# Issuing the gated linear attention's score products for two levels at a time

## The chip, the cores and the metric

The kernel runs on one core of one Trainium2 chip. The metric is the time of one execution on the device, in microseconds (us); the times given are medians of several runs.

## The reference

Two layers of an encoder on 256 tokens of width 2048. Each layer has one input projection, three groups of heads that work side by side, one output projection, and a gated MLP with a depthwise convolution. The change touches one group only, the gated linear attention (GLA): four heads with keys of 64 and values of 128, run forward and backward and added.

```python
def gla_direction(q, k, v, log_a):
    ...
    cum = jnp.cumsum(log_a.astype(F32).reshape(b, h, n, c, dk), axis=3)
    pair = jnp.where(lower[:, :, None],
                     jnp.exp(jnp.minimum(cum[..., :, None, :] - cum[..., None, :, :], 0.0)), 0.0)
    scores = jnp.einsum('bhnik,bhnjk,bhnijk->bhnij', q, k, pair.astype(q.dtype))
    intra = jnp.einsum('bhnij,bhnjv->bhniv', scores, v)
    ...
la_f = split_heads(jax.nn.log_sigmoid((ga_f @ gate_w[0] + gate_b[0])...) / GLA_TAU, GLA_HEADS)
o = gla_direction(q, k, v, la_f) + flip_t(gla_direction(flip_t(q), flip_t(k), flip_t(v), flip_t(la_b)))
```

So the score of a pair of tokens (i, j) is the product of q_i and k_j, weighted in each channel by the exponential of the summed log gates between them.

## The kernel before

**Slots.** All weights are read as a list of slots, one block of some 128 output columns each. For every slot the main loop (`for s in range(4, NS + 1)`) does the same: ScalarE (ACT) makes a rounded copy of a weight block that is needed three slots later (`split_hi`, line 176), VectorE (DVE) makes the remainder of a block that is needed two slots later (`split_lo`, line 184), TensorE (PE) multiplies this slot's block (lines 202 and 204 for the slots named rq, rk, dq, dk and others; 24 products on lines 218 to 220 for the slots gv, rv, dv), and the result is evacuated: ACT line 225 and DVE line 226 first, then, in the rq and rk slots, the rotary embedding (lines 394 to 401). The order in a layer is gv0 to gv3, ga, gq, gk, gq, gk, rq0, rq1, rk0, rk1, rv0 to rv3, dv0 to dv3, eight slots of dq and dk, and so on. In the first layer rk1 is slot 12, rv0 to rv3 are slots 13 to 16 and dv0 to dv2 are slots 17 to 19; the names are used below for both layers.

**Side tasks.** The heads' work lies in generators. `run_tasks` lets each active one go on to its next `yield`. GLA is an "early" task, so it makes one step at the head of a slot (`run_tasks(0, (True,))`, ahead of the splits and the slot's products) and one at its tail (`run_tasks(1)`, behind the products and behind the slot's evacuation). Others make their first step of a slot behind the splits. GLA counts 2 of the 3 places for active tasks; the tasks behind it in the list wait until it ends. In the first layer `decay_strips` runs beside it in slots 12 to 18 (lines 721 to 726).

**Order.** The schedule is the program's own order: each engine works through its instructions in the order in which the program issues them, and waits by semaphores for the other engines.

**GLA.** The scores are built in eight levels, with blocks of b = 1, 2, 4, ... 128 tokens. A level needs: `exps(b)`, two or four exponentials on ACT (lines 513 to 517) from four running sums, into the tiles `ea` and `eb`; two products on DVE, `ea = q*ea` (line 555) and `eb = k*eb` (line 557, not at b = 1); eight small products on PE into two banks (`scores`, line 539); and two predicated copies on DVE from those banks into `mm` (line 564; at b = 128 two copies on ACT, line 572). `update(b)`, four additions on DVE (line 524), makes the sums of the next level. One level takes two steps:

```python
                dve.tensor_mul(ea, q, ea)
                if b > 1:
                    dve.tensor_mul(eb, k, eb)
                yield
                bk = scores(k if b == 1 else eb, ea, b == P)
                if b < P:
                    update(b)
                    exps(2 * b)
```

The first `yield` of level 1 falls at the head of slot rk1, so the eight score blocks stand at the tails of rk1, rv0, ... dv2, one per slot. The final products (lines 584 and 587) follow.

Of the kernel before, what the change touches and what calls it, by code (L numbers as in the profile page):

```python
# [20 lines left out]
P = 128  # L21
T = 256
# [77 lines left out]
def encoder_kernel(ctx: ExitStack, tc: tile.TileContext, wflat, xT, par, con, masks, gate_w, lam_p, rel_bias, decay, out):  # L100
    nc = tc.nc
    pe, act, dve, pool = nc.tensor, nc.scalar, nc.vector, nc.gpsimd
# [7 lines left out]
    big = Slots(rot, "big", 36, 512)  # L110
# [247 lines left out]
    class Mixer:  # L358
# [98 lines left out]
        def gla(self):  # L457
# [3 lines left out]
            pf, sb, sfx, pbx = (big.get() for _ in range(4))  # L461
# [17 lines left out]
            for pr in range(2):  # L479
                act.activation(ab[pr], ab[pr], AF.Exp, scale=-1.0)  # L480
            yield
            q, k, ea, eb = (big.get() for _ in range(4))
            mm = [big.get() for _ in range(2)]
            for pr in range(2):
                for d, src in ((q, "gq"), (k, "gk")):
# [7 lines left out]
            bk, d = [banks.get() for _ in range(2)], tny.get()  # L493
# [15 lines left out]
            def V(a, b):  # L509
                return a.rearrange("p (n w b) -> p n w b", w=2, b=b)  # L510

            def exps(b):
                act.activation(V(ea, b)[:, :, 1], V(pf, b)[:, :, 1], AF.Exp, scale=1.0 / TAU)
                act.activation(V(ea, b)[:, :, 0], V(sb, b)[:, :, 0], AF.Exp, scale=1.0 / TAU)
                if b > 1:
                    act.activation(V(eb, b)[:, :, 0], V(sfx, b)[:, :, 0], AF.Exp, scale=1.0 / TAU)
                    act.activation(V(eb, b)[:, :, 1], V(pbx, b)[:, :, 1], AF.Exp, scale=1.0 / TAU)

            def update(b):
                n = 256 // b  # L520
                lo, up = (lambda a: V(a, b)[:, :, 0]), (lambda a: V(a, b)[:, :, 1])

                def add(dst, src):
                    dve.tensor_add(dst, dst, src.to_broadcast([P, n, b]) if b > 1 else src)  # L524

                add(lo(sfx), up(pf)[:, :, b - 1:b])
                add(up(pbx), lo(sb)[:, :, 0:1])
                add(up(pf), lo(pf)[:, :, b - 1:b])
                add(lo(sb), up(sb)[:, :, 0:1])

            def scores(ks, qs, cross):
                bk = [banks.get() for _ in range(2)]
                for pr in range(2):
                    for jb in range(2):
                        ib = 1 - jb if cross else jb
                        for hp in range(2):
                            rows = slice(64 * hp, 64 * hp + 64)
                            c = (pr * 2 + jb) * P
                            pe.matmul(bk[hp][:, c:c + P], lhsT=ks[rows, c:c + P],  # L539
                                      rhs=qs[rows, (pr * 2 + ib) * P:(pr * 2 + ib + 1) * P], start=True, stop=True)  # L540
                return bk

            for pr in range(2):
                for d, dst in ((0, pf), (1, sb)):
                    sl = slice(d * T, (d + 1) * T)
                    dve.scalar_tensor_tensor(dst[:, pr * T:(pr + 1) * T], zs[pr][:, sl], 0.0, ab[pr][:, sl],
                                             ALU.min, ALU.subtract)
            big.put(*zs, *ab)
            exps(1)
            yield  # L550
            yield
            b = 1
            lev = 0
            while b < T:
                dve.tensor_mul(ea, q, ea)
                if b > 1:
                    dve.tensor_mul(eb, k, eb)
                yield
                bk = scores(k if b == 1 else eb, ea, b == P)
                if b < P:  # L560
                    update(b)
                    exps(2 * b)
                    for hp in range(2):
                        dve.copy_predicated(
                            mm[hp].rearrange("p (n i) -> p n i", i=P),
                            mask_t[:, lev:lev + 1, :].to_broadcast([P, 4, P]),
                            bk[hp].rearrange("p (n i) -> p n i", i=P))
                else:
                    big.put(pf, sb, sfx, pbx, ea, eb, q, k)
                    mo = [big.get() for _ in range(2)]  # L570
                    for hp in range(2):
                        act.activation(mo[hp], bk[hp], AF.Copy)
                banks.put(*bk)
                yield
                b *= 2
                lev += 1
            for pr in range(2):
                yield
                po = banks.get()
# [345 lines left out]
    for s in range(4, NS + 1):  # L925
        l, kind, i, c, _ = slots[min(s, NS - 1)]
# [50 lines left out]
        else:  # L977
            b = banks.get()
# [134 lines left out]
```

## Time and profile before

| | us |
|---|---|
| median of 3 runs | 2320.37 (2320.01 to 2320.68) |
| the profiled execution | 2320.66 |
| its span, first to last instruction | 2318.9 |
| PE, DVE, ACT busy | 2293.3, 1705.8, 1236.9 |

The span is what the trace holds; the profiled execution's own time is 1.76 us longer. Busy time of PE is the time in which a matrix product was under way, and their ends are modelled. In a timeline a row gives start, length, engine, line, operation, the tiles written and read, shapes and how many were merged (xN); in brackets the idle time of the engine before it and what ended that.

### The profile page before, as it was taken

The page shows a single profiled execution, that of the slowest core. Times are in us where ns is not written, and L with a number is a line of the kernel's source. Part 1 is how long each engine was busy: PE and PEld are TensorE (multiplying, and loading weights), DVE is VectorE, ACT ScalarE, POOL GpSimd, SP SyncE. Part 2 cuts the span into 40 slices and gives each one's busy share as a digit, 9 for nine tenths or more (in the row PEclk, how much of TensorE's full clock was granted, in tenths as well). Part 3 has the DMA queues.
Part 4 walks back from the last instruction along what each step waited for, and adds up shares of the span by engine and source line. Part 5 has one row for each costly group of instructions (what it writes and reads, how often), then busy time and mean ns, then how long its engine had stood idle before and what let it go on. Part 6 is the DMA issues. An engine that isn't in the chain of part 4 may idle for free.

```text
span 2318.9 us, 32791 instructions
## 1 busy us (share of the span) xinstructions
PE 2293.3 (99%) x13250; PEld 2013.3 (87%) x13250; DVE 1705.8 (74%) x2459; ACT 1236.9 (53%) x1769; POOL 62.3 (3%) x77
## 2 busy tenths in 40 slices
PE   8999999999999999999999999999999999999998
PEld 7888888888888888888888889888888888888887
DVE  7978886777577766777669788767775777567764
ACT  6557655555345533555445666545543555345553
POOL 0001100000000000000000111000000000000000
PEclk9999999999999999999999999999999999999999
DMA  7454445554555555555554444555555554555553
GB/s 284 176 176 162 163 168 191 186 187 172 192 200 184 194 180 189 197 182 186 189 184 165 154 164 156 182 193 182 187 177 200 184 197 176 187 199 183 191 177 105
DMA packets 66646, 423.10 MB, mean 182 GB/s; under 512 B 7960, under 2 KB 10904, under 8 KB 28096
## 3 DMA queue, kind: packets, MB, share of 16 engines
q1 hardware_dynamic: 66352, 420.96, 51.2%
q8 instruction: 104, 1.70, 0.3%
q14 instruction: 46, 0.38, 0.1%
q10 hardware_dynamic: 144, 0.06, 0.0%
HBM read 417.83 MB, written 2.11 MB: 181 GB/s over the span
## 4 chain that ended last, share of the span: by engine, by line
PE 89%; DVE 9%; ACT 1%; POOL 1%; issue 0%; DMA 0%; ACTq 0%; SPq 0%; DVEq 0%; POOLq 0%
PE bank L202 52%; PE bank L204 28%; DVE wts L184 2%; PE bank L218 2%; PE bank L219 2%; PE bank L220 2%; POOL tny L354 1%; DVE sml L232 1%; DVE sml L226 1%; PE bank L539 0%; DVE tny L644 0%; DVE big L642 0%; DVE sml L424 0%; DVE big L524 0%; DVE big L658 0%
## 5 line engine op out<-in xcount | busy, mean ns | idle before, releaser
L202 PE MATMUL bank<-big,wts 128*128 128x512 f32 x5760 | 1383.9, 392 | 8.4 <-DVE big L816 7.8
L202 PEld LDWEIGHTS bank<-big,wts 128*128 128x128 f32 x5760 | 1058.4, 188 | 217.1 <-DVE big L816 10.4
L176 ACT ACTIVATE wts<-wts 128x2048 fp32r<-128x2048 f32 (+3 forms) x398 | 744.2, 1870 | 308.8 <-PE bank L202 266.8
L184 DVE TENSOR_TENSOR wts<-wts,wts 128x2048 fp32r<-128x2048 f32 (+3 forms) x398 | 888.5, 2233 | 12.7 <-PE bank L219 8.4
L204 PEld LDWEIGHTS bank<-big,wts 128*128 128x128 f32 x5760 | 739.7, 191 | 28.4
L204 PE MATMUL bank<-big,wts 128*128 128x256 f32 x5760 | 748.6, 283 | 0.0
L890 DVE TENSOR_TENSOR x<-bank,x 128x256 f32<-128x256 f32 x256 | 108.7, 425 | 246.9 <-PE bank L204 242.5
L226 DVE TENSOR_TENSOR sml<-sml,bank 128x256 f32<-128x256 f32 (+1 forms) x242 | 101.8, 421 | 196.2 <-ACT sml L225 195.8
L225 ACT ACTIVATE sml<-bank 128x256 f32<-128x256 f32 (+1 forms) x242 | 92.0, 381 | 159.4 <-PE bank L204 159.2
L815 ACT ACTIVATE big<-sml 128x256 fp32r<-128x256 f32 x88 | 36.7, 417 | 190.8 <-DVE sml L813 190.8
L810 ACT ACTIVATE sml<-sml 128x256 f32<-128x256 f32 x88 | 36.8, 418 | 159.3 <-DVE sml L803 159.3
L218 PE MATMUL bank<-wts,big 128*128 128x512 f32 x256 | 103.3, 404 | 5.8 <-ACT wts L166 5.8
L801 ACT ACTIVATE sml<-sml,conv_t 128x256 f32<-128x256 f32 x176 | 103.4, 588 | 5.7 <-DVE sml L232 5.7
L232 DVE TENSOR_TENSOR sml<-sml,sml 128x256 f32<-128x256 f32 (+1 forms) x230 | 97.9, 426 | 7.9
L219 PE MATMUL bank<-wts,big 128*128 128x512 f32 x256 | 101.3, 396 | 0.0
L220 PE MATMUL bank<-wts,big 128*128 128x512 f32 x256 | 100.9, 394 | 0.0
L802 DVE SCALAR_TENSOR_TENSOR sml<-sml,conv_t,sml 128x255 f32<-128x255 f32 x176 | 84.3, 479 | 8.6 <-ACT sml L801 8.6
L803 DVE SCALAR_TENSOR_TENSOR sml<-sml,conv_t,sml 128x255 f32<-128x255 f32 x176 | 85.3, 485 | 6.3
L291 ACT ACTIVATE sml<-x 128x256 f32<-128x256 f32 x80 | 31.8, 415 | 77.1 <-DVE x L890 77.1
L816 DVE TENSOR_TENSOR big<-sml,big 128x256 fp32r<-128x256 f32 x88 | 37.4, 426 | 42.6 <-ACT big L815 42.6
L218 PEld LDWEIGHTS bank<-wts,big 128*128 128x128 f32 x256 | 48.8, 191 | 17.1 <-ACT wts L166 5.8
L220 PEld LDWEIGHTS bank<-wts,big 128*128 128x128 f32 x256 | 48.8, 191 | 10.4
(147 smaller groups left out, 1034.5 us busy)
## 6 DMA issues: line engine op xcount, KB each, us to landing
wts<-wflat SPq DMA_DIRECT2D x300, 1024.0 KB, 4.8
wts<-wflat SPq DMA_DIRECT2D x64, 960.0 KB, 4.7
wts<-wflat SPq DMA_DIRECT2D x32, 896.0 KB, 4.6
wts<-wflat SPq DMA_DIRECT2D x18, 256.0 KB, 5.7
x<-xT SPq DMA_DIRECT2D x8, 256.0 KB, 5.9
out<-big SPq DMA_DIRECT2D x8, 256.0 KB, 3.9
strips<-dr SPq DMA_DIRECT2D x1, 1536.0 KB, 8.7
sml<-sml SPq DMA_DIRECT2D x32, 32.0 KB, 1.9
```

The source lines that it names most:

```text
L176: act.activation(R(hi), raw, AF.Copy)
L184: dve.tensor_sub(R(lo), raw, hi)
L202: pe.matmul(pt, lhsT=R(hi[:, j * P:(j + 1) * P]), rhs=R(acts[j]), start=k == 0, stop=False)
L204: pe.matmul(pt[:, T:], lhsT=R(lo[:, j * P:(j + 1) * P]), rhs=R(acts[j][:, :T]), start=False, stop=k == n - 1)
L218: pe.matmul(pts[tb], lhsT=al, rhs=R(hi[:, w]), start=k == 0, stop=False)
L219: pe.matmul(pts[tb], lhsT=ah, rhs=R(lo[:, w]), start=False, stop=False)
L220: pe.matmul(pts[tb], lhsT=ah, rhs=R(hi[:, w]), start=False, stop=k == KB - 1)
L225: act.activation(t[:m], pts[0][:m, T:], AF.Copy)
L226: dve.tensor_add(d[:m], t[:m], pts[0][:m, :T])
L232: dve.tensor_mul(d[:m], d[:m], rb[:m])
L801: act.activation(c, us, AF.Identity, scale=w[1], bias=w[3])
L890: dve.tensor_add(xb[i], pts[0][:, h * T:(h + 1) * T], xb[i])
```

## The change

Two pairs of tiles take the place of `ea` and `eb`. Four iterations handle two levels each, in three steps: the first makes the first level's products with q and k, then `update` and `exps` of the second level into the other pair of tiles; the second step makes the second level's products; the third issues the score products of both levels, sixteen into four banks, then `update` and `exps` of the next pair's first level, then the predicated copies of both levels. The loop has 12 yields in place of 16. Every arithmetic instruction of before is still there, once.

```diff
-            q, k, ea, eb = (big.get() for _ in range(4))
+            q, k = big.get(), big.get()
+            es = [(big.get(), big.get()) for _ in range(2)]
...
-            def exps(b):
+            def exps(b, ea, eb):
...
-            exps(1)
-            yield
-            yield
-            b = 1
-            lev = 0
-            while b < T:
-                dve.tensor_mul(ea, q, ea)
-                if b > 1:
-                    dve.tensor_mul(eb, k, eb)
-                yield
-                bk = scores(k if b == 1 else eb, ea, b == P)
+            exps(1, *es[0])
+            yield
+            yield
+
+            def take(b, lev, bk):
                 if b < P:
-                    update(b)
-                    exps(2 * b)
                     for hp in range(2):
                         dve.copy_predicated(
...
                 else:
-                    big.put(pf, sb, sfx, pbx, ea, eb, q, k)
-                    mo = [big.get() for _ in range(2)]
                     for hp in range(2):
                         act.activation(mo[hp], bk[hp], AF.Copy)
                 banks.put(*bk)
+
+            for lev in range(0, 8, 2):
+                b = 1 << lev
+                for i in range(2):
+                    ea, eb = es[i]
+                    dve.tensor_mul(ea, q, ea)
+                    if b << i > 1:
+                        dve.tensor_mul(eb, k, eb)
+                    if i == 0:
+                        update(b)
+                        exps(2 * b, *es[1])
+                    yield
+                bks = [scores(k if b << i == 1 else es[i][1], es[i][0], b << i == P) for i in range(2)]
+                if 2 * b < P:
+                    update(2 * b)
+                    exps(4 * b, *es[0])
+                else:
+                    big.put(pf, sb, sfx, pbx, *es[0], *es[1], q, k)
+                    mo = [big.get() for _ in range(2)]
+                for i in range(2):
+                    take(b << i, lev + i, bks[i])
                 yield
-                b *= 2
-                lev += 1
```

## Rows read from the trace of the kernel before

**Rows 1.** The page, busy time and share of the span.
```profile
PE 2293.3 (99%) x13250; PEld 2013.3 (87%) x13250; DVE 1705.8 (74%) x2459; ACT 1236.9 (53%) x1769; POOL 62.3 (3%) x77
```
**Rows 2.** Waits of PE: who, for whom, us in total, times, longest.
```profile
PE bank L202 <- DVE big L816: 7.8, 6, 1.5
...
PE bank L202 <- DVE big L428: 0.6, 2, 0.3
```
**Rows 3.** Windows: the first layer's GLA stretch, busy us (instructions) by engine.
```profile
core 0: us, PE busy (x) PEld busy (x) DVE busy (x) ACT busy (x) POOL busy (x), PEclk, DMA share, GB/s
...
85.00:133.00 48.00, 47.76 (x290) 38.19 (x290) 47.56 (x80) 25.45 (x42) 0.00 (x0) 1.00 0.45 161
```
**Rows 4.** Timeline, first layer, slot rk1 and its tail.
```profile
80.40 1.91 ACT L176 ACTIVATE wts<-wts 128x2048 fp32r<-128x2048 f32 x1
...
81.79 0.68 DVE L555 TENSOR_TENSOR big<-big,big 128x512 f32<-128x512 f32 x1
...
84.71 1.16 PE L539 MATMUL bank<-big,big 64*128 64x128 f32 x16
84.81 0.38 ACT L225 ACTIVATE sml<-bank 128x256 f32<-128x256 f32 x1 [2.50 <-PE bank L204]
85.23 0.42 DVE L226 TENSOR_TENSOR sml<-sml,bank 128x256 f32<-128x256 f32 x1 [0.56 <-ACT sml L225]
```
**Rows 5.** Timeline, first layer, the tail of rk1, rv0 and rv1.
```profile
87.16 0.75 DVE L524 TENSOR_TENSOR big<-big,big 128x256 f32<-128x256 f32 x2
...
91.15 0.39 PE L220 MATMUL bank<-wts,big 128*128 128x512 f32 x1
91.47 1.16 PE L539 MATMUL bank<-big,big 64*128 64x128 f32 x16
...
92.56 0.50 PE L218 MATMUL bank<-wts,big 128*128 128x512 f32 x1
...
92.89 0.39 PE L219 MATMUL bank<-wts,big 128*128 128x512 f32 x1
...
93.16 0.75 DVE L524 TENSOR_TENSOR big<-big,big 128x256 f32<-128x256 f32 x2
...
94.50 1.35 DVE L564 COPY_PREDICATED big<-mask_t,bank 128x512 f32<-128x512 uint32 x2
...
95.29 0.41 ACT L517 ACTIVATE big<-big 128x256 f32<-128x256 f32 x1
...
95.75 0.67 DVE L555 TENSOR_TENSOR big<-big,big 128x512 f32<-128x512 f32 x1
...
96.95 2.27 DVE L184 TENSOR_TENSOR wts<-wts,wts 128x2048 fp32r<-128x2048 f32 x1
...
99.15 0.40 DVE L721 TENSOR_SCALAR dstr<-big,lg 128x384 f32<-128x384 f32 x1
```
**Rows 6.** Timeline, first layer, slot dv1: when a score block follows DVE.
```profile
125.45 2.28 DVE L184 TENSOR_TENSOR wts<-wts,wts 128x2048 fp32r<-128x2048 f32 x1
...
125.59 1.16 PE L539 MATMUL bank<-big,big 64*128 64x128 f32 x16 [0.24 <-DVE big L557]
```
**Rows 7.** Timeline, second layer, slot rk1.
```profile
1229.22 0.68 DVE L555 TENSOR_TENSOR big<-big,big 128x512 f32<-128x512 f32 x1
...
1232.53 1.16 PE L539 MATMUL bank<-big,big 64*128 64x128 f32 x16
```
**Rows 8.** Timeline, first layer, the decay strips on DVE in slot rv2.
```profile
106.10 0.30 DVE L726 TENSOR_TENSOR dstr<-dstr,ident 128x128 f32<-128x128 f32 x1
106.30 0.43 DVE L721 TENSOR_SCALAR dstr<-big,lg 128x384 f32<-128x384 f32 x1
...
107.31 0.76 DVE L524 TENSOR_TENSOR big<-big,big 128x256 f32<-128x256 f32 x2
```
**Rows 9.** Timeline of the weight loads, the score block of rk1.
```profile
84.71 0.97 PEld L539 LDWEIGHTS bank<-big,big 64*128 64x128 f32 x16
```
**Rows 10.** Timeline of PE at the start of the kernel.
```profile
5.81 0.80 PE L218 MATMUL bank<-wts,big 128*128 128x512 f32 x1 [5.81 <-ACT wts L166]
...
12.25 0.40 PE L220 MATMUL bank<-wts,big 128*128 128x512 f32 x1
12.48 0.40 PE L218 MATMUL bank<-wts,big 128*128 128x512 f32 x1
```

## The prediction

> **What bounds the kernel now.** I read the page's busy times first: TensorE (PE) is busy for 2293.3 of 2318.9 us [rows 1]. Then the list of waits: after the start, PE waits for others for some 9 us in all, most of it in the MLP (line 816, longest 1.5 us), and 0.6 us at the output projection [rows 2]. So a stall of PE that the change adds is not taken back anywhere, and little is there to be won: the change neither adds nor removes arithmetic. Third, the windows: in the 48 us of the first layer in which the score blocks stand, VectorE (DVE) is busy for 47.56 us [rows 3]. There the two engines run neck and neck, and the question is whether the new order still lets DVE finish what PE asks for. For that I read the timeline around slot rk1.
>
> **What the order gives today.** Score block 1 starts on PE at 84.71, at the tail of rk1 [rows 4]; block 2 starts at 91.47, at the tail of rv0 [rows 5]. The products for block 2 are made by DVE between these two, behind the evacuation of rk1, while PE works through the 24 products of rv0. That slot of PE work is their cover: 91.47 - 84.71 = 6.76 us with the block in it. The change puts block 2 right behind block 1. The cover is gone, and PE's queue holds rv0 behind block 2.
>
> **Term 1, block 2.** In the first layer the new order has update(1) and exps(2) at the head of rk1, behind the product of level 1, which starts at 81.79 [rows 4]. A product pair takes 96.95 - 95.75 = 1.20, so one product 0.60; update 94.50 - 93.16 = 1.34; from the start of an update to the end of the last of the four exponentials 95.29 + 0.41 - 93.16 = 2.54 [rows 5].
> - The product ends at 82.39, so exps(2) ends at 84.93 on ScalarE (ACT).
> - Behind it in ACT's queue stands the weight copy (line 176), which began at 80.40 and now waits: 1.9 us [rows 4], to 86.83. Only then comes the evacuation of rk1 (line 225), which today starts at 84.81, right behind PE.
> - DVE's line 226 follows line 225 by 0.42 [rows 4]: 87.25. From line 226 to the end of the rotary work is 87.16 - 85.23 = 1.93 [rows 4, 5]: 89.18.
> - The pair of level 2: 1.20, to 90.38. PE follows DVE by 125.59 - 125.45 = 0.14 [rows 6]: block 2 starts at 90.5.
> - Block 1 lasts 92.56 - 91.47 = 1.09 [rows 5], so PE is free at 85.80. Stall: 4.7 us.
>
> DVE has time for the weight remainder (line 184) before 87.25 and is not held up by it. In the second layer the same chain starts at 1229.22 and PE is free at 1232.53 + 1.09 = 1233.62 [rows 7]: 1229.22 + 0.60 + 2.54 + 1.90 + 0.42 + 1.93 + 1.20 + 0.14 = 1237.95. Stall: 4.3 us. If the weight copy did not hold up the evacuation, DVE's own work would set the time, update 1.34 and remainder 2.20 (99.15 - 96.95 [rows 5]) ahead of line 226: about 3.4 and 3.1 us. If ACT and DVE had all ready, zero. I take the full chain, since both queues keep their order in every row.
>
> **Term 2, block 32.** Two levels now share 1.5 slots, where each had a slot of its own. From the end of DVE's pair 2 to the end of pair 32, DVE has: four updates, 5.36; the copies of levels 1, 2, 4 and 8, 95.75 - 94.50 = 1.25 each [rows 5], 5.0; three remainders, 6.6; four pairs, 4.8; a wait of 0.6, because pair 8 comes right behind update(4) and its exps (2.54 + 0.60 against 1.34 + 1.20). That is 22.4 us. The first layer adds two steps of the decay strips, 107.31 - 106.10 = 1.2 and, without the addition, 1.0 [rows 8]: 24.6. PE has in the same time, from block 2's start to block 16's end: block 2 and rv0, 6.76; rv1 without a block, 6.76 - 1.28 = 5.48 (the block takes 92.66 - 91.38, at a pace of 0.23 per product [rows 5]); blocks 4 and 8, 2.3; rv2, 5.48; block 16, 1.09: 21.1. DVE ends later: PE stalls for 24.6 - 21.1 = 3.5 us in the first layer and 22.4 - 21.1 = 1.3 us in the second. Without the 0.6 or with an overlap of the small steps it would be 2 and 0.
>
> Blocks 4, 8 and blocks 64, 128 should not wait. Pair 8 ends some 10.4 us behind pair 2 (1.34 + 2.5 + 2.2 + 1.2 + 1.34 + 0.6 + 1.2), PE comes to block 8 after 13.3. Pair 128 ends about 11.6 us behind pair 32 in the first layer, PE comes to block 128 after 13.2, though with the exponentials and a bank evacuation on ACT between, this is the nearest miss.
>
> **Term 3, joined blocks.** PE loses 91.47 - 91.15 - 0.23 = 0.09 going into a block and 92.89 - 92.56 - 0.23 = 0.10 coming out [rows 5]. That is the lower bound, 0.19, for a joined pair. The upper: sixteen weight loads start within 0.97 - 0.19 = 0.78 [rows 9] while the block costs 1.28, so 0.5. I take 0.3, as half of the pairs are torn by a stall anyway: 8 x 0.3 = 2.4 saved. The old wait of 0.24 at block 64 [rows 6] goes too.
>
> **Costed at nothing.** The two further pairs of tiles cost space, no work. Four banks at once: in the rv and dv slots two others are held, six of eight. GLA ends four steps, two slots, earlier, so the retention and attention tasks behind it start earlier; all they could win is the 0.6 us at the output projection [rows 2]; what they could lose, if they crowd DVE, I bound by the 1.3 us of term 2's smaller stall. No transfer is moved past another that PE waits for: weights are loaded five slots ahead.
>
> **Sum.** 4.7 + 4.3 + 3.5 + 1.3 - 2.4 - 0.2 = 11.2 us. The profiled execution would go from a span of 2318.9 to 2330.1 and from 2320.66 to 2331.9; the median shown is 0.29 lower, so 2331.6.
>
> **The clock.** At the start PE has been idle for 5.81 us, and its first 14 products take 12.25 - 5.81 = 6.44 us, while the next follows after 0.23 [rows 10]: the lower of the two levels, 1.2 GHz, then 2.4 GHz, at a loss of 6.44 - 14 x 0.23 = 3.2 us. Waits of up to 1.5 us [rows 2] come later at a granted clock of 1.00 in the window read [rows 3]. The new stalls of 4.7 and 4.3 lie between. The Trainium skill's "TensorE: Matmul & The Clock Gate", Part 1, says that the gate halves the clock again once the engine has sat idle and that sustained work has to win it back; no run here shows it for a wait of this length. By it the time would be that of rival A, by the rows alone that of the sum.
>
> **Rivals.**
> - A, the clock falls at both first stalls. 3.2 us each, but in the first layer about half is spent in term 2's wait for DVE: +1.7 and +2.7, so 2336.0. For it: both stalls are nearer to 5.8 than to 1.5. Against it: PE works at full pace on both sides of them.
> - B, term 1 alone: DVE makes up its backlog before block 32. 11.2 - 4.8 = 6.4, so 2326.8. For it: term 2 is the difference of two sums of 20 us and more.
> - C, not slower: block 2 does not wait. It decides whether pair 2 ends before block 1 does, 85.80 and 1233.62. Then term 2 goes too, as DVE has gained over 4 us, and what is left is the joining: -2.4 - 0.2 - 0.6, so 2317.2, inside the 0.2% that a measurement of this kernel can tell from no change. For it: PE hardly ever waits today. Against it: the rotary rows of rk1 stand between PE's last product and pair 2 on DVE.
>
> **How the numbers follow.** Forecast 0.52, A 0.23, B 0.10, C 0.12, and 0.03 for a gain that I don't see. 0.2% is 4.6 us: slower 0.85, same 0.12, faster 0.03. The forecast's own range is 2328 to 2334 (term 1 without the weight copy, term 3 at 0.19). The range of 8 in 10 is 2325.5 to 2337: it takes in B and A and leaves out C and a third fall of the clock.
>
> **What would show it.** In the trace of after: a wait of PE at line 539 for line 557 of 4 to 5 us at the tail of rk1 in both layers, a second one two slots later, behind rv2, of 3.5 and 1.3 us; line 225 of rk1 some 2 us late, behind line 176; the clock at those places. It is wrong if PE's waits at line 539 stay under 2 us, or if PE loses time anywhere behind dv0.

## The result and the profile after

The changed kernel takes 2336.35 us (median of 6 runs, 2335.66 to 2337.24) against 2320.22 for the kernel before on the same chip (6 runs): a ratio of 1.0071, interval 1.0060 to 1.0082, some 16.1 us slower. That is inside the range of 8 in 10 (2325.5 to 2337), but 4.8 us above the forecast of 2331.6 and outside the forecast's own range (2328 to 2334); it is the time that rival A gave (2336.0).

The list of PE's waits, of the changed kernel (line 540 is the score products, 572 the second product of a pair, 570 the first):

```profile
PE bank L540 <- DVE big L572: 12.0, 4, 4.6
PE bank L202 <- DVE big L826: 7.9, 6, 1.5
...
PE bank L202 <- DVE big L428: 0.6, 2, 0.3
```

The other waits are those of the kernel before within 0.1 us [rows 2]; the four waits at line 540 are new, 12.0 us. The timeline of the first layer at the tail of rk1, where [rows 4] and [rows 5] show the old order (line 525 is the update, 518 the last exponential):

```profile
80.85 0.68 DVE L570 TENSOR_TENSOR big<-big,big 128x512 f32<-128x512 f32 x1
81.45 0.76 DVE L525 TENSOR_TENSOR big<-big,big 128x256 f32<-128x256 f32 x2
...
83.59 0.43 ACT L518 ACTIVATE big<-big 128x256 f32<-128x256 f32 x1
83.74 1.16 PE L540 MATMUL bank<-big,big 64*128 64x128 f32 x16
83.92 1.90 ACT L176 ACTIVATE wts<-wts 128x2048 fp32r<-128x2048 f32 x1
85.72 0.36 ACT L225 ACTIVATE sml<-bank 128x256 f32<-128x256 f32 x1
86.11 0.42 DVE L226 TENSOR_TENSOR sml<-sml,bank 128x256 f32<-128x256 f32 x1 [1.03 <-ACT sml L225]
...
88.64 0.68 DVE L572 TENSOR_TENSOR big<-big,big 128x512 f32<-128x512 f32 x1
...
89.47 2.08 PE L540 MATMUL bank<-big,big 64*128 64x128 f32 x16 [4.57 <-DVE big L572]
...
91.48 0.79 PE L218 MATMUL bank<-wts,big 128*128 128x512 f32 x1
...
98.90 0.39 PE L218 MATMUL bank<-wts,big 128*128 128x512 f32 x1
```

Read it downwards: block 1 at 83.74, right behind the slot's products; ACT goes from the exponentials into the weight copy and only at 85.72 into the evacuation; DVE's pair of level 2 follows; block 2 has waited 4.57 us. And block 2 then takes 91.48 - 89.47 = 2.01 us where one took 1.09 [rows 5], and rv0 takes 7.42 us from its first product to that of rv1. The windows say why (the columns are those of [rows 3]; the last three are granted clock, DMA share and GB/s; a clock of 1.00 is the higher of the two levels, 0.50 the lower):

```profile
89.40:95.40 6.00, 5.93 (x25) 4.95 (x26) 6.00 (x10) 3.14 (x5) 0.00 (x0) 0.50 0.15 40
115.40:119.40 4.00, 3.94 (x22) 3.30 (x23) 4.00 (x9) 2.96 (x5) 0.00 (x0) 0.57 0.19 78
1246.40:1252.40 6.00, 5.95 (x25) 4.95 (x26) 6.00 (x10) 3.14 (x5) 0.00 (x0) 0.50 0.16 41
```

The granted clock is at the lower level, 0.50, behind three of the four waits (the 0.57 is the mean of a window that begins with the higher level). Beside the wait of 4.57 us, these are the others, in the order block 32 of the first layer, blocks 2 and 32 of the second:

```profile
115.47 1.72 PE L540 MATMUL bank<-big,big 64*128 64x128 f32 x16 [2.21 <-DVE big L572]
```
```profile
1246.45 2.08 PE L540 MATMUL bank<-big,big 64*128 64x128 f32 x16 [4.15 <-DVE big L572]
...
1271.33 1.16 PE L540 MATMUL bank<-big,big 64*128 64x128 f32 x16 [1.03 <-DVE big L572]
```

**The account.** Waits: 4.57 + 2.21 + 4.15 + 1.03 = 11.96, less the old one of 0.24 [rows 6], 11.72. Lower clock: in the first layer block 2 costs 2.01 - 1.09 = 0.92 more and rv0 7.42 - 5.58 = 1.84 more (5.58 is 5.48 without a block, plus 0.10 out of one); the same two in the second layer 0.92 and 1.91 (rv0 there from 1248.46 to 1255.95); block 32 and rv3 of the first layer 0.56 and 1.00 (rv3 from 117.12 to 123.70). Sum 7.15. The span grew from 2318.9 to 2334.5 us, by 15.6, and PE was 1.0 us ahead before any of this (block 1 starts at 83.74, before at 84.71 [rows 4]; at the start of the kernel its clock rose earlier, and by the second weight slot, at 13.56 for 14.53, the whole lead was there). So the change cost 16.6, and 11.72 + 7.15 - 16.6 = 2.3 us were saved by the joined blocks; this last figure is a remainder, not a reading.

### The profile page after: what moved, and what is told of

The parts are those of the page before. It is cut to its first block, busy times and chain, and to the rows that moved or that the text cites. A ratio compares the mean times of both kernels' runs of the same rounds, so it can differ in the third digit from the quotient of the medians.

```text
span 2334.5 us, 32812 instructions
## 1 busy us (share of the span) xinstructions
PE 2297.5 (98%) x13250; PEld 2017.7 (86%) x13250; DVE 1706.3 (73%) x2459; ACT 1237.7 (53%) x1769; POOL 66.3 (3%) x77
## 4 chain that ended last, share of the span: by engine, by line
PE 88%; DVE 9%; ACT 1%; POOL 1%; issue 1%; DMA 0%; ACTq 0%; SPq 0%; DVEq 0%; POOLq 0%
PE bank L202 50%; PE bank L204 27%; PE bank L218 3%; PE bank L219 2%; PE bank L220 2%; DVE wts L184 2%; POOL tny L354 1%; DVE sml L226 1%; DVE sml L232 1%; PE bank L540 1%; DVE tny L654 0%; DVE big L652 0%; DVE sml L424 0%; DVE big L668 0%; ACT wts L176 0%
## 5 line engine op out<-in xcount | busy, mean ns | idle before, releaser
L218 PEld LDWEIGHTS bank<-wts,big 128*128 128x128 f32 x256 | 49.9, 195 | 17.0 <-ACT wts L166 5.9
L354 POOL TENSOR_TENSOR tny<-tny,mhalf 128x2 f32<-128x2 f32 (+1 forms) x24 | 48.5, 2022 | 447.1 <-DVE tny L353 447.1
```

The lines of the kernel that those rows point to most:

```text
L218: pe.matmul(pts[tb], lhsT=al, rhs=R(hi[:, w]), start=k == 0, stop=False)
```

## The experiments

Two pairs of questions. First, are the waits one cause or two: the place of block 2 (right behind block 1 and behind rk1's evacuation) and the density (three steps for two levels in place of four)? Experiment 1 undoes both, 2 the density alone and 3 the place alone. Second, does the clock cost time of its own (experiment 4), and does the weight copy on ACT stretch the wait (experiment 5)? The sixth is the version that the first ones point to.

**1. Sixteen steps, blocks joined.**
```diff
+                yield
                 bks = [scores(k if b << i == 1 else es[i][1], es[i][0], b << i == P) for i in range(2)]
```


> One yield more ahead of the score products, so 16 steps as in the kernel before, and the sixteen products of two levels stand a whole slot behind the second level's pair. My theory (two levels in three steps take away the cover that a slot's products gave, and nothing else is wrong): no wait of the score products over 0.3 us in either layer, no fall of the clock, and the joined blocks save 8 x 0.3 us and the old wait of 0.24: 2320.2 - 2.6 = 2317.6, between 2317.0 and 2318.5. Rival (sixteen products in a row from four banks cost PE or DVE time by themselves): 2320 or more, with waits of PE behind the blocks or of DVE for banks.

Measured: 2317.68 us (11 runs) against 2319.73 (15 runs), ratio 0.9991, interval 0.9982 to 1.0000. PE's waits:
```profile
PE bank L202 <- DVE big L428: 0.9, 2, 0.6
...
PE bank L540 <- PE bank L540: 0.2, 1, 0.2
```
The score products' waits for DVE are gone and the clock does not fall (1.00 from 80 to 140 and from 1225 to 1300 us). Joined blocks and four banks cost nothing: it is the steps that make the changed kernel slow. One yield more takes the 16 us of loss away; the 2 us of gain that are left reach the edge of the interval, 1.0000.

**2. Sixteen steps, but block 2 left behind block 1.**
```diff
                     take(b << i, lev + i, bks[i])
                 yield
+                yield
```


> One yield more behind the predicated copies, so 16 steps, but block 2 still right behind block 1 at the tail of rk1. Theory of two separate causes (place of block 2; density of the steps): the waits for block 2 stay, 4.6 and 4.2 us, each with a fall of the clock worth 2.9 us; the waits for block 32 (2.2 and 1.0 us, and the second fall in the first layer) are gone: 2320.2 + 8.8 + 5.7 - 2.6 = 2332.1, between 2331 and 2333. Rival (density alone: twelve steps make DVE late everywhere): 2317.6, no wait at block 2.

Measured: 2333.18 us, ratio 1.0057 (1.0044 to 1.0071). The score blocks in the timeline, first layer, and two of the second:
```profile
84.38 1.16 PE L540 MATMUL bank<-big,big 64*128 64x128 f32 x16
90.08 2.08 PE L540 MATMUL bank<-big,big 64*128 64x128 f32 x16 [4.53 <-DVE big L572]
104.99 2.06 PE L540 MATMUL bank<-big,big 64*128 64x128 f32 x32
118.08 1.16 PE L540 MATMUL bank<-big,big 64*128 64x128 f32 x16
119.42 1.16 PE L540 MATMUL bank<-big,big 64*128 64x128 f32 x16 [0.17 <-PE bank L540]
```
```profile
1243.91 2.08 PE L540 MATMUL bank<-big,big 64*128 64x128 f32 x16 [4.15 <-DVE big L572]
...
1287.26 1.16 PE L540 MATMUL bank<-big,big 64*128 64x128 f32 x16 [1.15 <-DVE big L572]
```
The waits for block 2 are those of the changed kernel, those for block 32 are gone. So the place alone costs some 13 us, 0.2 more than the upper end that was expected, with two falls of the clock in the profiled run. The 1.15 us at block 128 of the second layer was not expected: there DVE makes the retention task's operands (lines 241 to 252, 1283.62 to 1285.8) right ahead of the pair.

**3. Twelve steps, but pair 2 early.** The idle step ahead of level 1 makes update(1) and exps(2), and the head of rk1 both pairs.
```diff
             exps(1, *es[0])
             yield
+            update(1)
+            exps(2, *es[1])
             yield
...
-                    if i == 0:
+                    if i == 0 and lev:
                         update(b)
                         exps(2 * b, *es[1])
-                    yield
+                    if lev:
+                        yield
+                if not lev:
+                    yield
+                    yield
```


> Twelve steps as in the changed kernel, but update(1) and exps(2) in the idle step ahead of level 1 and the pair of level 2 at the head of rk1, ahead of rk1's evacuation. Theory of the recorded rival C (block 2 is the root; with it early, DVE has gained over 4 us and block 32 doesn't wait): 2317.6, no wait over 0.3. Theory of density: the wait at block 2 is gone, but DVE is only 1.1 us earlier in both layers while PE is 7 us earlier, so the wait turns up again at blocks 8, 16 and 32: about 7 us in the first layer and 4.5 in the second, 2320.2 + 11.5 - 2.6 = 2329, and up to 2334 where the clock falls on the way.

Measured: 2333.49 us, ratio 1.0061 (1.0047 to 1.0074). The blocks, first layer, then second:
```profile
84.69 2.06 PE L540 MATMUL bank<-big,big 64*128 64x128 f32 x32
97.78 1.16 PE L540 MATMUL bank<-big,big 64*128 64x128 f32 x16
99.77 1.16 PE L540 MATMUL bank<-big,big 64*128 64x128 f32 x16 [0.83 <-DVE big L574]
107.95 1.16 PE L540 MATMUL bank<-big,big 64*128 64x128 f32 x16 [1.35 <-DVE big L574]
113.88 2.08 PE L540 MATMUL bank<-big,big 64*128 64x128 f32 x16 [4.77 <-DVE big L574]
```
```profile
1254.46 1.16 PE L540 MATMUL bank<-big,big 64*128 64x128 f32 x16 [0.42 <-DVE big L574]
1261.66 1.16 PE L540 MATMUL bank<-big,big 64*128 64x128 f32 x16 [0.38 <-DVE big L574]
1266.41 2.08 PE L540 MATMUL bank<-big,big 64*128 64x128 f32 x16 [3.58 <-DVE big L574]
```
The wait at block 2 is gone, and almost all of it comes back: 7.0 and 4.4 us at blocks 8, 16 and 32, 11.3 in all against 12.0. PE comes early to a DVE that is hardly earlier. So either cause alone is enough for a loss of some 13 us, and both together cost 16 and not 27: a wait at block 2 lets DVE catch up, and the wait at block 32 is the shorter for it (2.21 us in the changed kernel, 4.77 here).

**4. The waits filled.** Products that nothing reads stand between block 1 and block 2 and between block 16 and block 32.
```diff
-                bks = [scores(k if b << i == 1 else es[i][1], es[i][0], b << i == P) for i in range(2)]
+                bks = [scores(k if b == 1 else es[0][1], es[0][0], False)]
+                fill = {0: 16, 4: 5}.get(lev, 0)
...
+                    for j in range(fill):
+                        a = self.norm.acts[j]
+                        pe.matmul(fb, lhsT=R(a[:, :P]), rhs=R(a), start=True, stop=True)
...
+                bks.append(scores(es[1][1], es[1][0], 2 * b == P))
```


> The changed kernel with products that nothing reads between block 1 and block 2 (16 of 512 columns, 3.6 us) and between block 16 and block 32 (5, 1.1 us), so that PE works through most of each wait. Theory (the fall of the clock behind a wait costs time of its own): no stretch at the lower clock in the score slots, the wait for block 32 in the first layer grows to 3 us or more, filler included, and the time is 2331, between 2329.5 and 2332.5, 5.4 us less than the changed kernel's 2336.3. Rival (DVE sets the end anyway and the clock costs nothing): 2336 as before, with the waits grown by what the clock no longer takes.

Measured: 2331.60 us, ratio 1.0053 (1.0039 to 1.0067), 4.8 us less than the changed kernel (4.3 if each is taken against the kernel before on its own chip), with 42 products more. The fillers are line 583:
```profile
84.87 3.92 PE L583 MATMUL bank<-big 128*128 128x512 f32 x16
89.47 1.16 PE L540 MATMUL bank<-big,big 64*128 64x128 f32 x16 [0.68 <-DVE big L572]
...
110.41 1.43 PE L583 MATMUL bank<-big 128*128 128x512 f32 x5
114.02 1.43 PE L540 MATMUL bank<-big,big 64*128 64x128 f32 x16 [2.18 <-DVE big L572]
```
Block 2 starts at 89.47, the very time of the changed kernel, and its row now has 1.16 and not 2.08. The wait for block 32 has grown to 2.18 and 1.1 of filler: what the clock no longer takes, DVE takes in part. No fall was expected; one is left in the profiled run, and it stands behind this wait:
```profile
84.80:95.40 10.60, 9.92 (x57) 7.96 (x54) 9.50 (x18) 4.44 (x7) 0.00 (x0) 1.00 0.26 93
...
114.80:118.20 3.40, 3.40 (x15) 2.60 (x12) 3.40 (x7) 3.14 (x5) 0.00 (x0) 0.50 0.02 5
```

**5. exps(2) early, pair 2 in its place.** The first and the second hunk of experiment 3, without the yields moved.
```diff
             yield
+            update(1)
+            exps(2, *es[1])
             yield
...
-                    if i == 0:
+                    if i == 0 and lev:
```


> The changed kernel with update(1) and exps(2) one step earlier, in the idle step ahead of level 1; the pair of level 2 stays behind the evacuation of rk1. So the weight copy on ScalarE doesn't wait for exps(2) any more. Theory (the recorded chain: exps(2), weight copy, evacuation, rotary, pair): the evacuation's ACT instruction starts within 0.3 us of the last product of rk1 or of the weight copy, DVE's line 226 comes about 1.1 us earlier than in the changed kernel (then held by DVE's own weight remainder), and the wait for block 2 falls from 4.6 and 4.2 to about 3.4 and 3.1 us; the time falls by 1 to 3 us to 2333 to 2335, as DVE still sets when block 32 starts. Rival (the evacuation and the rotary rows alone set the wait): it stays at 4.6 and 4.2, time 2336.

Measured: 2331.29 us, ratio 1.0053 (1.0039 to 1.0067). The waits for block 2 are 3.97 and 3.55, between the two theories. The timeline of the first layer, block 1 at 84.76, and block 2 of the second:
```profile
84.34 1.89 ACT L176 ACTIVATE wts<-wts 128x2048 fp32r<-128x2048 f32 x1
86.14 0.36 ACT L225 ACTIVATE sml<-bank 128x256 f32<-128x256 f32 x1
86.54 0.42 DVE L226 TENSOR_TENSOR sml<-sml,bank 128x256 f32<-128x256 f32 x1 [0.44 <-ACT sml L225]
...
89.90 1.25 PE L540 MATMUL bank<-big,big 64*128 64x128 f32 x16 [3.97 <-DVE big L574]
```
```profile
1245.09 2.08 PE L540 MATMUL bank<-big,big 64*128 64x128 f32 x16 [3.55 <-DVE big L574]
```
DVE is behind in rk0 already, so the early update starts only one product earlier and the weight copy still stands ahead of the evacuation. The edit took away a third of the delay that it was meant to take; what it took, 0.6 us, PE's wait lost. That the evacuation starts as the copy ends is read in both kernels; how long the wait would be without any hold-up on ACT was not measured. The time fell by more than expected (2333 to 2335). The mean clock goes with it: 0.995 in the profiled run of 2334.9 and 0.997 in the three others, 2331.0 to 2331.6. Why the clock fell less in those three is open.

**6. Sixteen steps and the early pair.** Experiment 3 with one yield ahead of the score products.

> Sixteen steps as in the first experiment, and update(1), exps(2) and the pair of level 2 early, at the head of rk1 and the step before, so that nothing of GLA stands behind rk1's evacuation on DVE. Theory (the first experiment has no loss left but a wait of 0.2 us in the middle of block 16 and 32): 2317.4, no different from the first experiment within 0.5 us. Rival (DVE's lag of the first experiment still costs PE in the slots behind): 2316 or less.

Measured: 2316.45 us (11 runs) against 2320.26 (15 runs), ratio 0.9985, interval 0.9976 to 0.9994. No wait at the score line, and PE is never idle in either GLA stretch:
```profile
89.52 2.06 PE L540 MATMUL bank<-big,big 64*128 64x128 f32 x32
102.61 2.06 PE L540 MATMUL bank<-big,big 64*128 64x128 f32 x32
```
```profile
85.00:133.00 48.00, 48.00 (x303) 39.55 (x302) 47.79 (x76) 26.84 (x42) 0.00 (x0) 1.00 0.50 179
1230.00:1281.00 51.00, 51.00 (x320) 42.20 (x319) 48.15 (x70) 28.32 (x44) 0.00 (x0) 1.00 0.48 168
```
Two slots with a joined pair take 102.61 - 89.52 = 13.09 us; two slots with a block each took 2 x 6.76 = 13.52 [rows 4, 5]. A pair saves 0.43 us, eight of them 3.4, and the old wait 0.24: 3.7 of the 3.8 measured. This is the version whose interval lies clear of no change, and the joining accounts for the gain. Of the two expectations neither was met: 2317.4 is 0.95 too much, and the rival's 2316 too little. Experiment 1 joins the same blocks and gained 2.1 us; the two intervals overlap, so that the early pair adds to the gain is not shown.

## Why the prediction was right, and where it was not

**Term 1, block 2: right.** 4.57 and 4.15 us were measured for 4.7 and 4.3, with each link of the chain in the rows: exponentials, weight copy, evacuation, rotary work, pair. The reason given, that the cover of one slot's products is gone, is shown by experiments 1 and 2: both have sixteen steps, and the wait is there while block 2 stands right behind block 1 and gone once a slot's products lie between pair and block.

**Term 2, block 32: right in cause, too large in size.** 2.21 and 1.03 were measured for 3.5 and 1.3. From the end of pair 2 to the end of pair 32 these rows of DVE in the changed kernel count, each layer's first and last being the work right behind those pairs:

```profile
89.25 0.76 DVE L525 TENSOR_TENSOR big<-big,big 128x256 f32<-128x256 f32 x2
...
105.63 2.59 DVE L557 COPY_PREDICATED big<-mask_t,bank 128x512 f32<-128x512 uint32 x4 [1.38 <-PE bank L540]
...
115.24 0.75 DVE L525 TENSOR_TENSOR big<-big,big 128x256 f32<-128x256 f32 x2
```
```profile
1246.23 0.75 DVE L525 TENSOR_TENSOR big<-big,big 128x256 f32<-128x256 f32 x2
...
1262.68 2.59 DVE L557 COPY_PREDICATED big<-mask_t,bank 128x512 f32<-128x512 uint32 x4 [2.44 <-PE bank L540]
...
1271.10 0.75 DVE L525 TENSOR_TENSOR big<-big,big 128x256 f32<-128x256 f32 x2
```

That is 25.99 and 24.87 us. Without DVE's own waits of 1.38 and 2.44 for blocks 4 and 8 it is 24.6 and 22.4, as the sum has it. PE's side, 21.1, was too short: 23.7 and 23.8 were measured (block 16 starts at 112.09 and 1269.14), because the lower clock had stretched block 2 and rv0. That this makes DVE wait for PE in turn, and gives part of the time back, was not in the sum. With block 2's wait filled (experiment 4) the first layer takes 114.02 - 110.41 = 3.6 us from block 16 to block 32, filler and wait, for the 3.5 of the sum.

**Term 3, joined blocks: 0.3 per pair, measured 0.43** where the pair is not torn by a wait (experiment 6). In the changed kernel four of the eight pairs were torn, as the prediction had allowed for; its 2.4 stands against a remainder of 2.3, which is no reading.

**The clock: the step that failed.** The likeliest case put the clock behind the new stalls at nothing; there were three falls in the profiled run, and 7.15 us of lost pace stand behind them, some of it taken back by the shorter waits at block 32. Rival A had the mechanism and the size of its two falls: +1.7 and +2.7, where 2.76 us of lost pace less 1.3 of wait, and 2.83 less 0.3, make +1.5 and +2.5. That its 2336.0 met the time is partly luck: a third fall, 1.56 us behind block 32, was not in it, and was named as outside the range; in the profiled run PE's lead of 1.0 us from the start of the kernel took most of it back. The page "TensorE: Matmul & The Clock Gate" of the Trainium skill, Part 1, had the side of it that the trace now bears out: idle time takes the clock, and work has to win it back. The trace agrees: the clock is 0.50 behind the wait of 4.57 us, and 1.00 again in the window from 95.4 to 112, after block 2 and rv0's first nine products. Experiment 4 shows that this costs time by itself: the same stretch of 4.6 us, filled but for 0.68, is followed by full pace, and the kernel is 4.3 to 4.8 us faster for it. That it takes the 2331.6 which the forecast gave for no fall is chance, as one fall is left in its profiled run.

**Rival C was argued wrongly, though not needed.** It said that without the wait at block 2 term 2 goes too, as DVE has gained 4 us. It is PE that gains, not DVE; experiment 3 shows 11.3 us of waits left.

**Two readings of the prediction** don't hold as they stand, though no term hangs on them. PE's waits behind the start are 10.2 us in all by the whole list, not some 9. And the window of [rows 3] holds none of the waits of up to 1.5 us that it is quoted for; they lie in the MLP, where the window from 575 to 590, with a wait of 1.46 in it, has a clock of 1.00 as well. The 3.1 us for the second layer without the weight copy's hold-up should be 3.0.

**Costed at nothing: right.** No cost of the four banks, the further tiles or the two slots that GLA ends earlier shows: behind dv1 PE's waits are those of before within 0.1 us.

## What to carry to other kernels

When a change makes a stage of an interleaved side task take fewer steps, count the cover of each step: what the bounding engine waits for was made here while that engine did a slot of other work, and joining two uses must not remove that slot. Where two engines run neck and neck, a stall removed at one place comes back at the next unless the late engine itself has gained; ask which of the two the edit makes earlier. And price a stall of the tensor engine with the clock: in the profiled run of the changed kernel each of the three longest waits cost more than half its length again in lost pace behind it.

## What the runs showed of the hardware

- The granted clock fell to the lower level behind PE's waits of 4.57, 4.15 and 2.21 us in the changed kernel, 4.53 and 4.15 in experiment 2, 4.77 and 3.58 in experiment 3, 2.18 in experiment 4, 3.97, 3.55 and 2.21 in experiment 5; not behind those of 1.02 to 1.5. A score block of 1.09 us then takes 2.01. The falls differ from run to run: the four runs of experiment 5 have a mean clock of 0.995, 0.997, 0.997 and 0.997 and take 2334.9, 2331.0, 2331.6 and 2331.0 us.
- Going from the long products into a block of 64-row score products and out again costs PE 0.43 us more than going on within a block, though the same instructions run (13.09 us for two slots with a joined pair, 13.52 for two with a block each).
